# Neighbour sums by permutation matmuls: narrower one-hots in the first pass, and ten instead of eight destination blocks by row gathers

## The chip, the core and the metric

One core of a Trainium2 chip. The metric is device microseconds (us) of one execution. TensorE (PE in the profile) multiplies, VectorE (DVE) makes one-hot matrices by comparing keys with an index row, ScalarE (ACT) casts and empties PSUM (the memory that TensorE writes; the tiles that the other engines work on lie in SBUF), GpSimd (POOL) issues row gathers, and SyncE (SP) issues plain transfers.

## The reference, cut to what matters

```python
num_nodes, num_edges, dim = 4096, 65536, 128      # src, dst random node numbers
output = np.zeros((num_nodes, dim), dtype=np.float32)
for i in range(len(edge_index_src)):
    output[edge_index_dst[i]] += node_features[edge_index_src[i]]
```

## The kernel before: the parts that matter

Pass 1 sorts the edges into 32 destination blocks of 128 nodes. It does so in 24 lanes (six quads of four), each with 22 or 21 columns of 128 edges: it ranks the edges of a lane within their block, makes a one-hot of the rank (`p`), and moves each edge's code to the slot of its rank by matmuls. Then there are two ways to a destination block. Pass 2 sorts the edges of a block once more, by source block, builds for each source block a matrix of counts from two one-hots, and multiplies the 32 matrices by X; a turn of the main loop does this for one block and is called a slot. X is split into three bfloat16 terms side by side (`x3`, in DRAM `x3d`). The other way gathers, for every slot of pass 1, the row of `x3d`, and sums rows by one-hot matmuls. In the profile `psa` are the counts, `pso` the products with X, `psg` the sums of gathered rows, and `psr` the ranks of pass 2. Eight blocks go this way:

```python
KG = 8                          # blocks by gathers
GROUPS = (4, 4, 8, 8)           # the other 24, in groups of pass 2
GB = 6                          # row buffers

def gather(d, q):               # one unit: block d, quad q, four gathers
    t = xg.tile([P, 4, 3 * P], BF16, name="rows", tag="xg")
    for l in range(4):
        G.indirect_dma_start(out=t[:, l, :], out_offset=None, in_=x3d[:, :],
            in_offset=bass.IndirectOffsetOnAxis(ap=gidx[:, place(q).start + l, d:d + 1], axis=0))
# ... gather_sum: four matmuls of 128x384 into psg for each unit
def add_up(n):                  # gathers run at most GB units ahead of the sums
    while summed < min(n, ready):
        issue(summed + GB); gather_sum(*order[summed]); summed += 1
# ... the main loop: TensorE sums gathered units at the end of every slot
for slot, (g, i) in enumerate(flat_slots):
    n = n0 + (len(order) - n0) * (slot + 1) // slots
    # ... one-hots of the next slot on VectorE, steps of pass 2 of later groups
    for k in range(8):
        blocks(k, cur, a)                       # 4 matmuls, then a copy on ScalarE
        if prev is not None: product(k, prev[1], prev[2])   # 4 matmuls of 128x384
    # ...
    add_up(n)
finish()
for k in range(8): product(k, prev[1], prev[2])             # the last slot's products
```

At the start GpSimd zeroes those halves of the two `p2b` tiles that pass 2 never writes:

```python
p2b = [sb1.tile([P, NCH, P], BF16, name=f"p2b{i}") for i in range(2)]
for t in p2b:
    G.memset(t[:, :NH, 64:], 0.0)
    G.memset(t[:, NH:, :64], 0.0)
```

## Time and profile before

| | before |
|---|---|
| time, median (lowest to highest) | 368.02 us (366.36 to 368.76) |
| span of the profiled run | 366.4 us |
| busy PE / DVE / ACT / POOL | 82 / 78 / 44 / 61% |
| first gather starts, last gather ends | 49.19, 337.85 us |

The prediction below shows the lines, and reads them by stretch.

### The profile page before, as it was taken

The page shows a single profiled execution, that of the slowest core. Times are in us where ns is not written, and L with a number is a line of the kernel's source. Part 1 is how long each engine was busy: PE and PEld are TensorE (multiplying, and loading weights), DVE is VectorE, ACT ScalarE, POOL GpSimd, SP SyncE. Part 2 cuts the span into 40 slices and gives each one's busy share as a digit, 9 for nine tenths or more (in the row PEclk, how much of TensorE's full clock was granted, in tenths as well). Part 3 has the DMA queues.
Part 4 walks back from the last instruction along what each step waited for, and adds up shares of the span by engine and source line. Part 5 has one row for each costly group of instructions (what it writes and reads, how often), then busy time and mean ns, then how long its engine had stood idle before and what let it go on. Part 6 is the DMA issues. An engine that isn't in the chain of part 4 may idle for free.

```text
span 366.4 us, 8352 instructions
## 1 busy us (share of the span) xinstructions
PE 299.4 (82%) x3527; PEld 219.8 (60%) x3527; DVE 287.0 (78%) x476; ACT 160.2 (44%) x297; POOL 224.5 (61%) x225
## 2 busy tenths in 40 slices
PE   0768867656373597979989999997799999999996
PEld 0557746535351466756667767675477676767663
DVE  4982899999759689699994799659994959687721
ACT  2778733300000373525534553545345555464650
POOL 5677048787877777706887768578437575775000
PEclk9978988978565699989999999999899999999999
DMA  8400922233232233310324323232213332332000
GB/s 245 114 2 2 311 74 73 69 73 79 62 79 77 75 80 81 91 29 13 82 64 99 87 75 75 64 86 67 70 36 85 72 86 72 90 85 71 26 9 21
DMA packets 22694, 27.96 MB, mean 76 GB/s; under 512 B 3776, under 2 KB 19328, under 8 KB 22656
## 3 DMA queue, kind: packets, MB, share of 16 engines
q0 software_dynamic: 9216, 18.89, 21.2%
q1 hardware_dynamic: 13296, 8.01, 7.6%
q8 instruction: 27, 0.44, 0.5%
q10 hardware_dynamic: 144, 0.52, 0.4%
q14 instruction: 11, 0.09, 0.1%
HBM read 22.02 MB, written 5.39 MB: 75 GB/s over the span
## 4 chain that ended last, share of the span: by engine, by line
PE 55%; DVE 36%; ACT 5%; DMA 1%; issue 1%; DVEq 0%
PE pso L530 27%; DVE oh L196 10%; PE psa L524 9%; DVE p L196 8%; PE psg L325 6%; PE ps L496 4%; DVE cum L465 3%; DVE v L257 3%; DVE oh L442 3%; PE psr L474 3%; PE psb L449 2%; ACT cum L236 2%; DVE v L456 2%; PE psr L241 1%; ACT x L178 1%; DVE cum L470 1%
## 5 line engine op out<-in xcount | busy, mean ns | idle before, releaser
L306 POOL DMA_INDIRECT rows<-x3d,gidx x192 | 199.8, 1041 | 101.2 <-issue 48.1
L530 PE MATMUL pso<-x,a 128*128 128x384 bf16 x768 | 156.3, 328 | 5.5 <-DVE res L333 5.5
L526 ACT CAST a<-psa 128x512 bf16<-128x512 f32 x192 | 112.1, 586 | 77.5 <-PE psa L524 77.0
L530 PEld LDWEIGHTS <-a 128*128 128x128 bf16 x768 | 67.8, 98 | 32.1 <-issue 6.5
L524 PE MATMUL psa<-oh 128*128 128x128 bf16 x768 | 74.3, 220 | 1.2 <-ACT a L526 0.9
L524 PEld LDWEIGHTS <-oh 128*128 128x128 bf16 x768 | 59.0, 98 | 26.1 <-issue 2.5
L196 DVE TENSOR_TENSOR oh<-psi,slo 128x4096 bf16<-128x4096 uint16 x24 | 54.7, 2281 | 10.0 <-PE psa L524 10.0
L196 DVE TENSOR_TENSOR oh<-psi,dlo 128x4096 bf16<-128x4096 uint16 x24 | 54.7, 2278 | 0.0
L325 PE MATMUL psg<-rows,ohg 128*128 128x384 bf16 x192 | 40.2, 353 | 4.5 <-DMA rows<-x3d,gidx 3.0
L196 DVE TENSOR_TENSOR p<-psi,rank 128x2688 bf16<-128x2688 uint16 (+1 forms) x24 | 36.1, 1566 | 0.0
L325 PEld LDWEIGHTS <-ohg 128*128 128x128 bf16 x192 | 19.0, 104 | 17.1 <-DVE ohg L196 4.7
L504 DVE TENSOR_SCALAR slo<-pa 128x128 uint16<-128x128 uint16 x12 | 3.0, 252 | 32.8 <-ACT pa L500 32.8
L236 ACT ACTIVATE cum<-psc,minus 128x512 bf16<-128x512 f32 (+1 forms) x36 | 22.0, 656 | 12.2 <-PE psc L233 11.8
L182 POOL TENSOR_TENSOR xf<-xf,x 128x512 f32<-128x512 f32 x16 | 19.8, 1275 | 11.3 <-ACT x L178 11.3
L196 DVE TENSOR_TENSOR p2b<-psi,rank 128x768 bf16<-128x768 uint16 x48 | 23.3, 545 | 2.3 <-ACT rank L479 2.3
L280 PE MATMUL psm<-v,p 128*128 128x64 bf16 x512 | 20.6, 200 | 4.9 <-DVE p L196 4.8
L449 PE MATMUL psb<-oh,before 128*128 128x128 bf16 (+1 forms) x96 | 12.3, 309 | 14.7 <-DVE oh L442 11.8
L280 PEld LDWEIGHTS <-p 128*128 128x128 bf16 x512 | 18.6, 103 | 6.9 <-DVE p L196 6.5
L496 PEld LDWEIGHTS <-p2b 128*128 128x128 bf16 x576 | 19.7, 101 | 3.6 <-DVE p2b L196 2.1
L333 DVE TENSOR_REDUCE res<-pso 128x128 f32<-128x384 f32 x24 | 13.1, 546 | 10.0 <-PE pso L530 10.0
L233 PEld LDWEIGHTS <-sums 128*128 128x128 bf16 x126 | 12.1, 116 | 14.4 <-issue 6.6
L449 PEld LDWEIGHTS <-before 128*128 128x128 bf16 x96 | 10.0, 127 | 17.2 <-DVE oh L442 12.7
(72 smaller groups left out, 255.2 us busy)
## 6 DMA issues: line engine op xcount, KB each, us to landing
x3d<-x SPq DMA_DIRECT2D x4, 768.0 KB, 4.8
rows<-x3d,gidx POOLq DMA_INDIRECT x192
xf<-in_node_features_dram SPq DMA_DIRECT2D x4, 512.0 KB, 7.9
out_dram<-res SPq DMA_DIRECT2D x32, 64.0 KB, 1.9
raw<-in_edge_index_src_dram ACTq DMA_DIRECT2D x1, 512.0 KB, 5.2
raw<-in_edge_index_dst_dram SPq DMA_DIRECT2D x1, 512.0 KB
x3d<-zrow SPq DMA_DIRECT2D x1, 96.0 KB, 5.7
x3d<-zrow SPq DMA_DIRECT2D x1, 48.0 KB
```

Of the source, the lines that this page charges most:

```text
L182: G.tensor_tensor(out=xf[i][:, bs], in0=xf[i][:, bs], in1=part[:, bs], op=OP.add)
L196: V.tensor_tensor(out=dst.rearrange("p i (m k) -> p i m k", k=2), in0=io.rearrange("p i (m k) -> p i m k", k=2), in1=keys2[:, :, None, :]. ...
L236: S.activation(out=cum[:, :, 4 * j0:4 * (j0 + n)], func=RELU, bias=minus[:], in_=psc[:, :n * P].rearrange("p (t b) -> p b t", b=NB))
L280: PE.matmul(out=psm[:, l * 64:(l + 1) * 64], lhsT=p1[:, l % 2, j, :], rhs=v1[q][:, 4 * j + l].rearrange("p k b -> p (k b)"), start=j == 0, ...
L306: G.indirect_dma_start(out=t[:, l, :], out_offset=None, in_=x3d[:, :], in_offset=bass.IndirectOffsetOnAxis(ap=gidx[:, place(q).start + l, ...
L325: PE.matmul(out=psg[d][:, :3 * P], lhsT=oh[:, l, :], rhs=t[:, l, :], start=q == 0 and l == 0, stop=q == NQ - 1 and l == 3)
L333: V.tensor_reduce(out=res[:], in_=pso[:, :3 * P].rearrange("p (v f) -> p f v", v=3), op=OP.add, axis=AX.X, negate=True)
L449: PE.matmul(out=psb[:, h * W:(h + 1) * W], lhsT=before[:], rhs=flat2(oh2)[:, h * NH + c], start=c == 0, stop=c == NH - 1)
L496: PE.matmul(out=ps2[:, d % 2 * NB:(d % 2 + 1) * NB], lhsT=p2b[d % 2][:, c, :], rhs=v2[:, c, d // kk, :, d % kk], start=c == 0, stop=c == N ...
L524: PE.matmul(out=psa[:, i * P:(i + 1) * P], lhsT=oh[0][:, s, :], rhs=oh[1][:, s, :], start=True, stop=True)
L526: S.copy(out=a[:, k * 4:k * 4 + 4, :], in_=psa[:].rearrange("p (s m) -> p s m", s=4))
L530: PE.matmul(out=pso[:, :3 * P], lhsT=a[:, s, :], rhs=x3[:, s, :, :].rearrange("p v f -> p (v f)"), start=s == 0, stop=s == NB - 1)
```

## The change

The intent: compare only those ranks that a column of a lane can reach, and shift two blocks from TensorE and VectorE to GpSimd, which looks free. The prediction also weighs casts of X on ScalarE; the diff doesn't touch them. The diff, cut to its core (the rest rewrites pass 2 from generators to lists of steps with the same operations, and counts edges for the fallback's flag in another way):

```diff
-KG = 8
-GROUPS = (4, 4, 8, 8)
+KG = 10
+GROUPS = (4, 4, 8, 6)
+WIN = ((0, 7, 0, 64), (7, 14, 4, 100), (14, NJ, 20, P))
 ...
+    p1 = [sb1.tile([P, 2, NJ, P], BF16, name=f"p1{i}", tag=f"t2{i}") for i in range(2)]
+    for t in p1:
+        for j0, j1, m0, m1 in WIN:
+            if m0 > 0:
+                G.memset(t[:, :, j0:j1, :m0], 0.0)
+            if m1 < P:
+                G.memset(t[:, :, j0:j1, m1:], 0.0)
 ...
-            onehot(p1[:, l % 2, :n], rank1[q][:, l, :n], n)
+            for j0, j1, m0, m1 in WIN:
+                j1 = min(j1, n)
+                onehot(t[:, l % 2, j0:j1, m0:m1], rank1[q][:, l, j0:j1], j1 - j0, m1 - m0, m0=m0)
 ...
+                if l == 1 and q > 0:
+                    scan(q + 2)
+                if l > 0 or q == 0:
+                    count(q + 2, 2 if l < 3 else 99)
 ...
-        if q + 3 < NQ:
-            scan(q + 3)
```

More of the change, by code (lines that the diff above doesn't have):

```diff
@@ L25 @@
 BIG = 4096.0
-KG = 8
-GROUPS = (4, 4, 8, 8)
-STEPS = {0: [(1, 2)], 1: [(1, 2)], 2: [(1, 0)], 3: [(1, 0), (2, 1)], 4: [(2, 2)], 5: [(2, 1)],
-         6: [(2, 0)], 7: [(2, 0)], 9: [(2, 0), (3, 1)], 11: [(2, 0)], 12: [(3, 2)], 13: [(3, 1)],
-         14: [(3, 0)], 16: [(3, 0)], 18: [(3, 0)], 20: [(3, 0)]}
+KG = 10
+GROUPS = (4, 4, 8, 6)
+STEPS = {0: [(1, 2)], 1: [(1, 2)], 2: [(1, 1)], 3: [(1, 1), (2, 1)], 4: [(2, 2)], 5: [(2, 1)],
+         6: [(2, 1)], 7: [(2, 1)], 9: [(2, 1), (3, 1)], 11: [(2, 1)], 12: [(3, 2)], 13: [(3, 1)],
+         14: [(3, 1)], 16: [(3, 1)], 18: [(3, 1)]}
+WIN = ((0, 7, 0, 64), (7, 14, 4, 100), (14, NJ, 20, P))
 GE = 2
@@ L116, in _fast @@
     minus = sb1.tile([P, 1], F32, name="minus")
+    one = sb1.tile([P, 1], F32, name="one")
     iota = sb1.tile([P, P], U16, name="iota")
@@ L126, in _fast @@
     G.memset(minus[:], -BIG)
+    G.memset(one[:], 1.0)
     G.iota(iota[:], pattern=[[1, P]], base=0, channel_multiplier=0)
@@ L191, in _fast, with onehot @@
     oh1, sums, rank1, v1 = {}, {}, {}, {}
-    def onehot(dst, keys2, n, m=P, io=None):
-        io = (piota if io is None else io)[:, None, :m].to_broadcast([P, n, m])
+    def onehot(dst, keys2, n, m=P, io=None, m0=0):
+        io = (piota if io is None else io)[:, None, m0:m0 + m].to_broadcast([P, n, m])
         V.tensor_tensor(
@@ L273, in move1 @@
         for l in range(4):
-            if l % 2 == 0:
-                p1 = sb2.tile([P, 2, NJ, P], BF16, name="p1", tag="t2")
+            t = p1[l // 2]
             n = len([j for j in range(NJ) if j * NCH + q * 4 + l < T])
-            onehot(p1[:, l % 2, :n], rank1[q][:, l, :n], n)
+            for j0, j1, m0, m1 in WIN:
+                j1 = min(j1, n)
+                onehot(t[:, l % 2, j0:j1, m0:m1], rank1[q][:, l, j0:j1], j1 - j0, m1 - m0, m0=m0)
             meanwhile(l)
             for j in range(n):
-                PE.matmul(out=psm[:, l * 64:(l + 1) * 64], lhsT=p1[:, l % 2, j, :],
+                PE.matmul(out=psm[:, l * 64:(l + 1) * 64], lhsT=t[:, l % 2, j, :],
                           rhs=v1[q][:, 4 * j + l].rearrange("p k b -> p (k b)"),
@@ L393, in step @@
             if q + 2 < NQ:
-                count(q + 2, 2 if l < 3 else 99)
+                if l == 1 and q > 0:
+                    scan(q + 2)
+                if l > 0 or q == 0:
+                    count(q + 2, 2 if l < 3 else 99)
             if q == 0:
@@ L426, in pass2 @@
         shape = [P, NCH, gk, NB, kk]
-        if g == 0:
-            both = sb1.tile([P, 2] + shape[1:], BF16, name="vc2", tag="o0")
-            v2, cum2 = both[:, 0], both[:, 1]
-            oh2 = sb1.tile(shape, BF16, name="oh2", tag="o1")[:]
-        else:
-            oh2 = sb1.tile(shape, BF16, name="oh2", tag="c0")[:]
-            v2 = sb1.tile(shape, BF16, name="v2", tag="c1")[:]
-            cum2 = sb1.tile(shape, BF16, name="cum2", tag="o1")[:]
-        ds = slice(d0, d0 + gd)
         W = NB * gd
+        T2 = {}
@@ L438, in flat2 @@
         def flat2(t):
             return t.rearrange("p c i s k -> p c (i s k)")
-        for s in range(NB):
-            V.tensor_single_scalar(
-                out=oh2[:, :, :, s, :], in_=sbk[:, :, ds].rearrange("p c (i k) -> p c i k", k=kk),
-                scalar=float(s + 1), op=OP.is_equal)
-        yield
-        psb = ps.tile([P, 512], F32, name="psb", tag="misc", bufs=1)
-        for h in range(2):
-            for c in range(NH):
-                PE.matmul(out=psb[:, h * W:(h + 1) * W], lhsT=before[:],
-                          rhs=flat2(oh2)[:, h * NH + c], start=c == 0, stop=c == NH - 1)
@@ L451, in pass2 @@
-        for h in range(2):
-            S.copy(out=flat2(cum2)[:, h * NH], in_=psb[:, h * W:(h + 1) * W])
-        yield
-        for i in range(gk):
-            V.tensor_tensor(out=v2[:, :, i], in0=oh2[:, :, i], op=OP.mult,
-                            in1=sa[:, :, None, d0 + kk * i:d0 + kk * i + kk].to_broadcast(
-                                [P, NCH, NB, kk]))
-        yield
-        yield
-        cums = flat2(cum2).rearrange("p (h c) w -> p h c w", h=2)
-        ohs2 = flat2(oh2).rearrange("p (h c) w -> p h c w", h=2)
@@ L464, in pass2 @@
-        for c in range(1, NH):
-            V.tensor_tensor(out=cums[:, :, c], in0=cums[:, :, c - 1], in1=ohs2[:, :, c - 1],
-                            op=OP.add)
-        yield
-        yield
-        V.tensor_tensor(out=flat2(cum2), in0=flat2(cum2), in1=flat2(oh2), op=OP.mult)
-        yield
-        psr = ps.tile([P, 512], F32, name="psr2", tag="misc", bufs=1)
-        for s in range(NB):
-            PE.matmul(out=psr[:, :NCH * gd], lhsT=identb[:],
-                      rhs=cum2[:, :, :, s, :].rearrange("p c i k -> p (c i) k"),
-                      start=s == 0, stop=s == NB - 1)
@@ L477, in pass2, with tiles @@
-        rank2 = sb2.tile([P, gd, NCH, 2], BF16, name="rank2")
-        for k in range(2):
-            S.copy(out=rank2[:, :, :, k],
-                   in_=psr[:, :NCH * gd].rearrange("p (c d) -> p d c", d=gd))
-        yield
-        pa = sb2.tile([P, gd, NB], BF16, name="pa")
-        slo2 = sb2.tile([P, gd, NB, 2], U16, name="slo2")
-        dlo2 = sb2.tile([P, gd, NB, 2], U16, name="dlo2")
-        keys2[g] = (slo2, dlo2)
-        for i in range(0, gd, 2):
+        def tiles():
+            if g == 0:
+                both = sb1.tile([P, 2] + shape[1:], BF16, name="vc2", tag="o0")
+                T2["v"], T2["c"] = both[:, 0], both[:, 1]
+                T2["o"] = sb1.tile(shape, BF16, name="oh2", tag="o1")[:]
+            else:
+                T2["o"] = sb1.tile(shape, BF16, name="oh2", tag="c0")[:]
+                T2["v"] = sb1.tile(shape, BF16, name="v2", tag="c1")[:]
+                T2["c"] = sb1.tile(shape, BF16, name="cum2", tag="o1")[:]
@@ new lines, in buckets, with before_all @@
+        def buckets():
+            tiles()
+            ds = slice(d0, d0 + gd)
+            for s in range(NB):
+                V.tensor_single_scalar(
+                    out=T2["o"][:, :, :, s, :], scalar=float(s + 1), op=OP.is_equal,
+                    in_=sbk[:, :, ds].rearrange("p c (i k) -> p c i k", k=kk))
+        def before_all():
+            psb = ps.tile([P, 512], F32, name="psb", tag="misc", bufs=1)
+            for h in range(2):
+                for c in range(NH):
+                    PE.matmul(out=psb[:, h * W:(h + 1) * W], lhsT=before[:],
+                              rhs=flat2(T2["o"])[:, h * NH + c], start=c == 0, stop=c == NH - 1)
+            for h in range(2):
+                S.copy(out=flat2(T2["c"])[:, h * NH], in_=psb[:, h * W:(h + 1) * W])
@@ new lines, in payloads, with running @@
+        def payloads():
+            for i in range(gk):
+                V.tensor_tensor(out=T2["v"][:, :, i], in0=T2["o"][:, :, i], op=OP.mult,
+                                in1=sa[:, :, None, d0 + kk * i:d0 + kk * i + kk].to_broadcast(
+                                    [P, NCH, NB, kk]))
+        def running():
+            cums = flat2(T2["c"]).rearrange("p (h c) w -> p h c w", h=2)
+            ohs2 = flat2(T2["o"]).rearrange("p (h c) w -> p h c w", h=2)
+            for c in range(1, NH):
+                V.tensor_tensor(out=cums[:, :, c], in0=cums[:, :, c - 1], in1=ohs2[:, :, c - 1],
+                                op=OP.add)
@@ new lines, in masked, with ranks @@
+        def masked():
+            V.tensor_tensor(out=flat2(T2["c"]), in0=flat2(T2["c"]), in1=flat2(T2["o"]), op=OP.mult)
+        def ranks():
+            psr = ps.tile([P, 512], F32, name="psr2", tag="misc", bufs=1)
+            for s in range(NB):
+                PE.matmul(out=psr[:, :NCH * gd], lhsT=identb[:],
+                          rhs=T2["c"][:, :, :, s, :].rearrange("p c i k -> p (c i) k"),
+                          start=s == 0, stop=s == NB - 1)
+            T2["r"] = sb2.tile([P, gd, NCH, 2], BF16, name="rank2")
+            for k in range(2):
+                S.copy(out=T2["r"][:, :, :, k],
+                       in_=psr[:, :NCH * gd].rearrange("p (c d) -> p d c", d=gd))
@@ L488, in pass2, with permutations @@
+        def permutations(i):
+            if i == 0:
+                T2["pa"] = sb2.tile([P, gd, NB], BF16, name="pa")
+                keys2[g] = [sb2.tile([P, gd, NB, 2], U16, name=n) for n in ("slo2", "dlo2")]
             for d in range(i, i + 2):
@@ L490, in pass2, with permuted @@
                     cs = slice(h * NH, (h + 1) * NH)
-                    onehot(p2b[d % 2][:, cs, h * 64:h * 64 + 64], rank2[:, d, cs], NH, 64)
-            yield
+                    onehot(p2b[d % 2][:, cs, h * 64:h * 64 + 64], T2["r"][:, d, cs], NH, 64)
+        def permuted(i):
             ps2 = ps.tile([P, 512], F32, name="ps2", tag="misc", bufs=1)
@@ L496, in pass2, with pair_keys @@
                     PE.matmul(out=ps2[:, d % 2 * NB:(d % 2 + 1) * NB],
-                              lhsT=p2b[d % 2][:, c, :], rhs=v2[:, c, d // kk, :, d % kk],
+                              lhsT=p2b[d % 2][:, c, :], rhs=T2["v"][:, c, d // kk, :, d % kk],
                               start=c == 0, stop=c == NCH - 1)
-            ds = slice(i, i + 2)
-            S.copy(out=pa[:, ds], in_=ps2[:, :2 * NB].rearrange("p (d s) -> p d s", d=2))
-            yield
-            pau = pa[:, ds].bitcast(U16).rearrange("p d s -> p (d s)")[:, :, None].to_broadcast(
-                [P, 2 * NB, 2])
-            V.tensor_single_scalar(out=slo2[:, ds].rearrange("p d s k -> p (d s) k"), in_=pau,
-                                   scalar=7, op=OP.logical_shift_right)
-            V.tensor_single_scalar(out=dlo2[:, ds].rearrange("p d s k -> p (d s) k"), in_=pau,
-                                   scalar=127, op=OP.bitwise_and)
+            S.copy(out=T2["pa"][:, i:i + 2],
+                   in_=ps2[:, :2 * NB].rearrange("p (d s) -> p d s", d=2))
+        def pair_keys(i):
+            pau = T2["pa"][:, i:i + 2].bitcast(U16).rearrange("p d s -> p (d s)")[
+                :, :, None].to_broadcast([P, 2 * NB, 2])
+            for t, arg, op in zip(keys2[g], (7, 127), (OP.logical_shift_right, OP.bitwise_and)):
+                V.tensor_single_scalar(out=t[:, i:i + 2].rearrange("p d s k -> p (d s) k"),
+                                       in_=pau, scalar=arg, op=op)
             if i == 0:
-                V.tensor_reduce(out=fmax[:, NQ + g:NQ + 1 + g], in_=rank2[:, :, :, 0], op=OP.max,
+                V.tensor_reduce(out=fmax[:, g:g + 1], in_=T2["r"][:, :, :, 0], op=OP.max,
                                 axis=AX.XY)
-            yield
+        pairs = [tuple(lambda f=f, i=i: f(i) for f in (permutations, permuted, pair_keys))
+                 for i in range(0, gd, 2)]
+        return [(buckets, before_all), (payloads,), (running,), (masked, ranks)] + pairs
     def onehots(g, i):
-        oh = sb2.tile([P, 2, NB, P], BF16, name="oh", tag="t2")
+        oh = sb1.tile([P, 2, NB, P], BF16, name="oh", tag=f"t2{(first[g] + i) % 2}")
         for k, io in ((0, piotas), (1, piota)):
@@ L534, in flag @@
     def flag():
-        for q in range(NQ):
-            V.tensor_reduce(out=fmax[:, q:q + 1], in_=rank1[q][:, :, :, 0], op=OP.max, axis=AX.XY)
-        V.tensor_single_scalar(out=fmax[:, :NQ], in_=fmax[:, :NQ], scalar=-64.0, op=OP.add)
+        ng = len(GROUPS)
+        full = sb1.tile([P, NCH * NB], BF16, name="full", tag="o2")
+        V.tensor_single_scalar(out=full[:], in_=sbk[:].rearrange("p c b -> p (c b)"), scalar=0.5,
+                               op=OP.is_gt)
+        V.tensor_reduce(out=fmax[:, ng:ng + 1], in_=full[:], op=OP.add, axis=AX.X)
@@ L539, in flag @@
+        V.tensor_scalar(out=fmax[:, :ng], in0=fmax[:, :ng], scalar1=63.5, scalar2=float(2 * P * T),
+                        op0=OP.is_gt, op1=OP.mult)
         fall = sb1.tile([P, 1], F32, name="fall")
-        V.tensor_reduce(out=fall[:], in_=fmax[:, :NQ + len(GROUPS)], op=OP.max, axis=AX.X)
+        V.tensor_reduce(out=fall[:], in_=fmax[:, :ng + 1], op=OP.add, axis=AX.X)
         psf = ps.tile([P, 512], F32, name="psf", tag="misc", bufs=1)
-        PE.transpose(out=psf[:1, :P], in_=fall[:], identity=ident[:])
@@ L543, in flag @@
-        fone = sb1.tile([1, 1], F32, name="fone")
-        V.tensor_reduce(out=fone[:], in_=psf[:1, :P], op=OP.max, axis=AX.X)
-        V.tensor_single_scalar(out=flag_i[:], in_=fone[:], scalar=63.5, op=OP.is_gt)
-    gens = [pass2(g) for g in range(len(GROUPS))]
-    def on(g):
-        next(gens[g])
-    pending = []
-    on(0)
-    on(0)
-    serve(NQ - 1)
-    for _ in range(2):
-        on(0)
-        on(0)
-    on(0)
-    on(0)
-    add_up(8)
-    on(0)
-    on(0)
-    ready = len(order)
@@ L566, in _fast, with run @@
-    on(0)
-    prepare(10)
-    on(0)
-    oh = onehots(0, 0)
-    on(0)
-    add_up(10)
-    on(0)
-    prev = None
+        PE.matmul(out=psf[:1, :1], lhsT=fall[:], rhs=one[:], start=True, stop=True)
+        V.tensor_single_scalar(out=flag_i[:], in_=psf[:1, :1], scalar=float(P * T),
+                               op=OP.not_equal)
+    todo = [pass2(g) for g in range(len(GROUPS))]
+    def run(fs):
+        for f in fs:
+            f()
+    run(todo[0].pop(0))
+    serve(NQ - 1)
+    for _ in range(3):
+        run(todo[0].pop(0))
@@ L574, in _fast @@
+    add_up(9)
+    vec, mat, keys = todo[0].pop(0)
+    vec()
+    mat()
+    ready = len(order)
+    prepare(12)
+    keys()
+    vec, mat, keys = todo[0].pop(0)
+    vec()
+    oh = onehots(0, 0)
+    mat()
+    keys()
+    add_up(12)
+    prev = None
+    pending = []
     n0 = summed
@@ L577, in _fast @@
     for slot, (g, i) in enumerate(flat_slots):
-        steps = STEPS.get(slot, ())
         n = n0 + (len(order) - n0) * (slot + 1) // slots
-        for pg in pending:
-            on(pg)
-        pending = [pg for pg, k in steps if k == 0]
+        run(pending)
+        steps = [todo[pg].pop(0) for pg, k in STEPS.get(slot, ()) for _ in range(k)]
+        pending = [f for st in steps for f in st[2:]]
         prepare(n)
@@ L586, in _fast @@
             oh = onehots(*flat_slots[slot + 1])
-        for pg, k in steps:
-            for _ in range(max(k - 1, 0)):
-                on(pg)
-                on(pg)
-            on(pg)
+        run(st[0] for st in steps)
         finish()
@@ L600, in _fast @@
             done.append((prev[0], prev[2]))
-        for pg, k in steps:
-            on(pg)
+        run(st[1] for st in steps if len(st) > 1)
         add_up(n)
```

## The prediction

> **What bounds the kernel now.** I read the chain that ended last first, to see which engine sets the end; then the stretches of 20 us, to see where each engine is full; then GpSimd's timeline, because the change gives GpSimd a quarter more of its one long job.
>
> The page's busy shares and chain:
>
> ```profile
> PE 299.4 (82%) x3527; PEld 219.8 (60%) x3527; DVE 287.0 (78%) x476; ACT 160.2 (44%) x297; POOL 224.5 (61%) x225
> ...
> PE 55%; DVE 36%; ACT 5%; DMA 1%; issue 1%; DVEq 0%
> ```
>
> TensorE carries over half of the chain, VectorE a third, GpSimd nothing. The stretches (busy us of PE, PEld, DVE, ACT, POOL, then clock, DMA share, GB/s):
>
> ```profile
> 60.00:80.00 20.00, 11.76 (x231) 9.51 (x232) 19.73 (x24) 4.96 (x12) 15.73 (x15) 0.85 0.30 74
> 100.00:120.00 20.00, 11.31 (x138) 7.57 (x135) 14.87 (x26) 0.83 (x4) 15.14 (x16) 0.59 0.33 80
> 300.00:320.00 20.00, 20.00 (x212) 14.22 (x210) 16.32 (x18) 10.89 (x20) 13.33 (x15) 1.00 0.30 80
> ```
>
> So pass 1 (about 38 to 86 us) is VectorE's, the setup of pass 2 (to about 115) is latency with no full engine, and from about 200 us TensorE has no gap. GpSimd shows 13 to 16 of 20 us and looks free. It isn't quite; the groups and its timeline say why:
>
> ```profile
> L306 POOL DMA_INDIRECT rows<-x3d,gidx x192 | 199.8, 1041 | 101.2 <-issue 48.1 <-PE psg L325 34.3 <-DVE gkey L296 12.4
> ```
>
> ```profile
> 49.19 1.10 POOL L306 DMA_INDIRECT rows<-x3d,gidx  x1 [12.40 <-DVE gkey L296]
> ...
> 155.46 0.95 POOL L306 DMA_INDIRECT rows<-x3d,gidx  x1 [0.30 <-issue]
> 167.53 4.51 POOL L306 DMA_INDIRECT rows<-x3d,gidx  x1 [11.12 <-PE psg L325]
> ...
> 181.47 3.94 POOL L306 DMA_INDIRECT rows<-x3d,gidx  x1 [0.30 <-issue]
> 185.72 0.95 POOL L306 DMA_INDIRECT rows<-x3d,gidx  x1 [0.30 <-issue]
> 186.97 0.94 POOL L306 DMA_INDIRECT rows<-x3d,gidx  x1 [0.30 <-issue]
> ```
>
> A gather is 0.95 us plus a gap of 0.30 that nothing fills: one every 1.25 us, and the gap is not counted as busy. The stream begins at 49.19 and ends at 337.85, 288.7 us. It splits into 191 steps of 1.25 plus a last 0.95 (239.7), 18 us by which some gathers were longer than 0.95 (my sum over all of them), and some 31 us of waits for TensorE to free a row buffer (11.1, 8.9 and seven small ones). Those 31 us and the 17 us from the last unit's bytes to the matmuls that use it (340 to 357) are all the slack that GpSimd has.
>
> **What the Trainium skill says.** "SBUF — State Buffer", section "SBUF: two separate sides", says that VectorE and GpSimd share a port pair as an exclusive lock, and that while VectorE runs an instruction that holds it, GpSimd cannot write DMA descriptors. The trace agrees: VectorE's mask multiply (L470, 128x6144, all in SBUF) runs from 181.25 to 184.60, and the gather begun at 181.47 takes 3.94 instead of 0.95. The one-hot compares, whose index row lies in PSUM, leave gathers at 0.95. "Perfetto Trace Analysis", section "DMA Instruction — SWDGE (GPSIMD)", says that such an instruction's recorded end is the last descriptor, not the data: here the queues move bytes until about 158.0 after a gather that ended at 156.41, and until about 340 after 337.85, so rows land 1.6 to 2.1 us later. "TensorE: Matmul & The Clock Gate", section "Part 1: The HAM clock gate", has the clock halve after an idle window of about 3.4 us and come back after as much work; here TensorE's idle 159.7 to 162.1 is followed by a granted clock of 0.50 from 163 to 166.
>
> **The change part by part.**
>
> *Pass 1 one-hots.* 24 compares of 2816 or 2688 elements (means 1611 and 1544 ns; four back to back take 5.84, so 1.46 apiece in pace) become 72 over windows of 7x64, 7x96 and 8x108: 1984 elements, or 1876 where there are 21 columns, about 70%. From the paces of the 4096- and 2688-element compares (2.20 and 1.46) an element costs 0.526 ns and an instruction about 0.06 us fixed. The three cost 1876 x 0.526 + 0.18 = 1.17, so 0.3 is saved per lane, 1.2 per quad, 7 us in the six. Quad 0's is hidden behind ScalarE; about 6 us lie on VectorE's path. I worked out every slot of the drawn edges from the reference's inputs: ranks are 0 to 49, 14 to 84 and 35 to 110 in the three windows, so none falls outside and the fallback isn't taken.
>
> *Scans.* VectorE sits 7.4 us before the scan at 37.60, waiting for column sums that TensorE reaches only after quad 0. Moved into the next quad after its second compare, the scan lets two of quad 1's four compares run in that hole, some 2.5 to 3.4 us. Later quads hardly wait there (0.25).
>
> *Zeroing the windows' margins.* 3328 elements on GpSimd in 16 memsets; by p2b's 0.73 for 768 about 3.4 us, in a stretch where it idles 3.35 before the first subtraction. No cost.
>
> *Casts of X.* The diff leaves them as they are, already 12 ScalarE instructions of 1.07 us. Nothing.
>
> *The flag.* Six reduces (1.0 us) become a compare and a reduce over 768. Even.
>
> *Two blocks from products to gathers.* Slots go from 24 to 22. Each slot removed takes from TensorE 8 x 0.87 = 7.0 us (psa and pso); the pair takes one permutation (1.5 us) too: 15.5. Added are 48 matmuls of 128x384 at 0.163: 7.8. Net 7.7 us less in a stretch where TensorE is full. VectorE loses 8.8 of slot one-hots, 1.9 of p2b and a quarter of the last group's work, and gains 12 x 0.37.
>
> So TensorE and VectorE alone would bring 367.7 to about 367.7 - 6 - 3 - 7.7 = 351. But GpSimd gets 48 more gathers, 60 us at 1.25, against 48 us of slack, of which the faster engines take away more. So its stream should set the end:
> - Start: the first gather needs x3d written. The writes fill the queues until 47.1 (329 GB/s at 45) and are bound by bandwidth, so 49.2 becomes about 47, not less.
> - 240 gathers without a wait: 239 x 1.25 + 0.95 = 299.7.
> - Longer gathers behind VectorE's port: 18 us now. Instructions that fell in GpSimd's waits (the 192-element bucket compares at 158, the multiply at 264) will now hit a running stream, the last group is a quarter smaller: about 19.
> - So the last gather ends at 47 + 299.7 + 19 = 365.7, and lands at 367.7.
> - The tail: from the last four psg matmuls (357.20) to the end of the span (366.4) is 9.2 now, with the final 32 products behind them: 376.9.
> - In the last slot TensorE waits for three units at 5 us each, so the final products should start at half clock: 1.8 more, 378.7.
> - Measured times lie 1.3 to 1.8 above the span: about 380. I take 379.
>
> Do the buffers keep the stream from stalling? Gather units per slot go from 38/24 = 1.6 to 48/22 = 2.2, so 8.7 gathers or 10.9 us a slot, against TensorE's 7.0 + 0.75 + 2.2 x 0.65 = 9.2. Through the first slots, where TensorE now takes 10 to 12, the stream is six buffers ahead: unit 24, say, is issued near 177 and needs unit 18 summed, done before 166 in today's slot 3. So I expect hardly a wait for TensorE, and TensorE waiting instead.
>
> **The rivals.** (a) *TensorE stays the bound*: 351. For it: the chain shows no GpSimd, and its busy share is 61%. Against it: the share leaves out the 0.30 gaps, and even with no blocked gather 47 + 299.7 + 11.2 + 1.5 = 359.4 is a floor. (b) *Fewer blocked gathers*: if the rearranged VectorE stream meets only 12 us of them and the clock holds, 370, within 2%. For it: how much one such instruction costs varied from 0.6 (multiply at 77.58) to 3.6 us (167.5). (c) *The half clock spreads*: if the per-slot wait of about 2 us grew past some 2.5, each slot's matmuls would slow, but the gathers leave room for that, so it adds a few us at most: 383 to 386. (d) *The fallback runs*: many times slower, ruled out by the ranks unless the count is wrong.
>
> **Range and chances.** The certain part is 299.7 + 11.2 + 1.5 = 312.4; the start (46 to 49), blocking (14 to 23) and final clock (0 to 2) give 372 to 386. I take 371 to 386. Slower than 375.1 (2%) needs start plus blocking plus final clock above 62.7, where I expect 67: 0.80. Faster than 360.4 needs almost no blocking: 0.02.
>
> **What would show it.** Right: GpSimd's gathers at 1.25 us without a wait from about 47 to 366, waits for psg near zero, TensorE idle before psg for rows in most slots from the sixth on, the chain of waits with GpSimd in it, the 72 compares taking about 29 us of VectorE against 36.1 now, final products at a clock under 1. Wrong: gathers closer than 1.25, a stream that still waits for TensorE, TensorE full after 200 us, or an end near 351.

## The result, and the profile after

The changed kernel takes 388.18 us (385.48 to 390.54, 4 runs) against 368.02: slower. The ratio is 1.055, with a 95% interval of 1.046 to 1.065. Ratios here are the mean time of one kernel's runs over that of the other's of the same rounds, so not quite the ratio of the medians. Executions over 1.5% slower than the fastest of the same kernel are left out of the means. All runs are correct; the fallback was not taken.

The direction and the mechanism were as predicted, but the time lies 2.2 us above the top of the range. The four runs fall in two pairs, 385.48 and 386.12, 390.23 and 390.54, and the profile is of the third. The page's busy shares and the chain that ended last (followed back from the last instruction, at each step to what released it), after:

```profile
PE 308.1 (79%) x3400; PEld 217.5 (56%) x3400; DVE 275.4 (71%) x522; ACT 150.2 (39%) x280; POOL 280.1 (72%) x282
...
PE 50%; DVE 15%; POOL 11%; issue 9%; DMA 9%; ACT 6%; ACTq 0%; DVEq 0%
```

GpSimd, its gaps ("issue") and the gathers' transfers, which had 2% of the chain, now have 29%, and VectorE's 36% have become 15%. The stretches (busy us of PE, PEld, DVE, ACT, POOL, then clock, DMA share, GB/s):

```profile
60.00:80.00 20.00, 13.09 (x229) 10.12 (x227) 17.04 (x38) 4.95 (x12) 15.74 (x14) 0.88 0.29 70
...
240.00:260.00 20.00, 15.43 (x106) 9.48 (x106) 10.23 (x12) 6.43 (x11) 15.13 (x17) 0.83 0.37 88
...
300.00:320.00 20.00, 20.00 (x248) 14.37 (x245) 14.67 (x22) 9.78 (x18) 15.13 (x17) 1.00 0.36 87
320.00:340.00 20.00, 16.54 (x142) 11.00 (x141) 13.07 (x14) 9.13 (x16) 15.12 (x17) 1.00 0.38 89
```

VectorE does have less to do in pass 1 (17.0 of 20 us against 19.7), but TensorE is no longer full in every stretch after 200 us. GpSimd shows 15.1 us in stretch after stretch: 16 gathers at 1.25 us fill 20 us, and 16 x 0.947 = 15.15 is what counts as busy. So 15.1 of 20 is a GpSimd that has no time left. The groups and who waited for whom, in two views:

```profile
L320 POOL DMA_INDIRECT rows<-x3d,gidx x240 | 250.8, 1045 | 83.6 <-issue 62.1
```

```profile
POOL rows L320 <- issue: 62.1, 204, 0.3
...
PE psg L339 <- DMA rows<-x3d,gidx: 29.9, 37, 1.9
```

The entry "PE psg 34.3" of before is gone from the gathers' row: GpSimd does not wait for TensorE any more. In its place TensorE waits 29.9 us for gathered rows.

Along GpSimd's stream the two kernels can be compared term by term. "Longer gathers" is the sum over all gathers of what they take above 0.948 us, and "waits" the sum of idle time above 0.30 before gathers other than the first:

| us | before | after | predicted for after |
|---|---|---|---|
| first gather starts | 49.19 | 51.36 | 47 |
| gathers and gaps alone | 239.8 | 299.8 | 299.7 |
| longer gathers | 18.1 | 23.7 | 19 |
| waits | 30.8 | 0.1 | 0 |
| last gather ends (the sum) | 337.85 | 375.00 | 365.7 |
| from there to the end of the span | 28.6 | 13.5 | 13.0 |
| span | 366.4 | 388.5 | 378.7 |

The 48 more gathers cost 60.0 us. The waits (30.7) and the slack at the end (15.1) gave 45.8 of that back; the start (2.2) and the longer gathers (5.6) added. That makes 22 us of span. Two terms were mis-sized, the start by 4.4 us and the longer gathers by 4.7.

**The start.** VectorE's first instructions, before and then after:

```profile
5.90 0.57 DVE L157 TENSOR_SCALAR kd<-raw 128x176 uint16<-128x176 uint16 x3 [2.88 <-DMA raw<-in_edge_index_dst_dram]
6.39 1.62 DVE L196 TENSOR_TENSOR oh<-psi,kd 128x2816 bf16<-128x2816 uint16 x1
7.92 0.42 DVE L163 TENSOR_SCALAR raw<-raw 128x528 uint16<-128x528 uint16 x1
```

```profile
5.87 1.87 DVE L170 TENSOR_SCALAR kd<-raw 128x176 uint16<-128x176 uint16 x3 [2.81 <-DMA raw<-in_edge_index_dst_dram]
7.67 1.60 DVE L209 TENSOR_TENSOR oh<-psi,kd 128x2816 bf16<-128x2816 uint16 x1
9.19 1.32 DVE L176 TENSOR_SCALAR raw<-raw 128x528 uint16<-128x528 uint16 x1
```

The same three shifts take 1.87 us instead of 0.57, and the next key operation 1.32 instead of 0.42. GpSimd's memsets at that time:

```profile
6.03 0.83 POOL L153 MEMSET p2b<- 128x768 bf16 x1
6.81 0.83 POOL L154 MEMSET p2b<- 128x768 bf16 x1
7.59 0.83 POOL L153 MEMSET p2b<- 128x768 bf16 x1
8.37 0.73 POOL L154 MEMSET p2b<- 128x768 bf16 x1
```

The new memsets come first, so the old ones, which used to end at 5.68 just before the keys arrived, now lie on top of VectorE's shifts. The one-hot compare, whose index row is in PSUM, takes its 1.60 as before. The delay then runs on: ScalarE makes the codes at 12.12 instead of 9.12, and the first write of `x3d` is issued at 38.49 instead of 35.91.

### The profile page after: what moved, and what is told of

It is laid out like the page before. It is cut to its first block, busy times and chain, and to the rows that moved or that the text cites. A ratio compares the mean times of both kernels' runs of the same rounds, so it can differ in the third digit from the quotient of the medians.

```text
span 388.5 us, 8206 instructions
## 1 busy us (share of the span) xinstructions
PE 308.1 (79%) x3400; PEld 217.5 (56%) x3400; DVE 275.4 (71%) x522; ACT 150.2 (39%) x280; POOL 280.1 (72%) x282
## 4 chain that ended last, share of the span: by engine, by line
PE 50%; DVE 15%; POOL 11%; issue 9%; DMA 9%; ACT 6%; ACTq 0%; DVEq 0%
PE pso L552 22%; POOL rows L320 11%; PE psa L546 8%; DMA rows<-x3d,gidx 8%; PE psg L339 5%; ACT cum L249 3%; DVE oh L209 3%; DVE p L209 2%; PE psr L254 2%; PE ps L515 2%; PE psb L470 2%; PE psr L494 2%; DVE oh L462 2%; PE psm L294 2%; PE psc L246 2%
## 5 line engine op out<-in xcount | busy, mean ns | idle before, releaser
L320 POOL DMA_INDIRECT rows<-x3d,gidx x240 | 250.8, 1045 | 83.6 <-issue 62.1
L552 PE MATMUL pso<-x,a 128*128 128x384 bf16 x704 | 150.7, 341 | 3.3 <-DVE res L347 3.3
L548 ACT CAST a<-psa 128x512 bf16<-128x512 f32 x176 | 102.6, 585 | 120.4 <-PE psa L546 118.0
L339 PE MATMUL psg<-rows,ohg 128*128 128x384 bf16 x240 | 55.8, 352 | 35.0 <-DMA rows<-x3d,gidx 29.9
L209 DVE TENSOR_TENSOR oh<-psi,slo 128x4096 bf16<-128x4096 uint16 x22 | 50.2, 2282 | 14.2 <-PE psa L546 14.2
L209 DVE TENSOR_TENSOR oh<-psi,dlo 128x4096 bf16<-128x4096 uint16 x22 | 50.1, 2279 | 0.0
L339 PEld LDWEIGHTS <-ohg 128*128 128x128 bf16 x240 | 23.5, 102 | 46.6 <-issue 30.9
L209 DVE TENSOR_TENSOR p<-psi,rank 128x448 bf16<-128x448 uint16 (+3 forms) x72 | 29.2, 479 | 0.0
L209 DVE TENSOR_TENSOR ohg<-psi,gkey 128x512 bf16<-128x512 uint16 x60 | 22.1, 412 | 0.0
L242 PE MATMUL psc<-oh,early 128*128 128x512 bf16 (+1 forms) x36 | 14.9, 414 | 3.2 <-ACT cum L249 3.2
```

The costliest lines, as they stand in the source:

```text
L209: V.tensor_tensor(out=dst.rearrange("p i (m k) -> p i m k", k=2), in0=io.rearrange("p i (m k) -> p i m k", k=2), in1=keys2[:, :, None, :]. ...
L242: PE.matmul(out=psc[:, :n * P], lhsT=early[:], rhs=oh1q(q)[:, 4 * j0:4 * (j0 + n), :].rearrange("p t b -> p (t b)"), start=True, stop=j0 + ...
L339: PE.matmul(out=psg[d][:, :3 * P], lhsT=oh[:, l, :], rhs=t[:, l, :], start=q == 0 and l == 0, stop=q == NQ - 1 and l == 3)
L548: S.copy(out=a[:, k * 4:k * 4 + 4, :], in_=psa[:].rearrange("p (s m) -> p s m", s=4))
L552: PE.matmul(out=pso[:, :3 * P], lhsT=a[:, s, :], rhs=x3[:, s, :, :].rearrange("p v f -> p (v f)"), start=s == 0, stop=s == NB - 1)
```

## The experiments

Ten kernels ran, all with correct results. Times are medians of all runs, with the ratio to the kernel before of the same rounds.

| run | what | time | ratio (95% interval) |
|---|---|---|---|
| e1_rest_only | the change without the two blocks | 362.67 | 0.985 (0.980 to 0.990) |
| e2_gathers_only | the two blocks without the rest | 385.05 | 1.044 (1.038 to 1.050) |
| e3_zero_later | change, p2b zeroed later | 383.74 | 1.041 (1.036 to 1.046) |
| e4_last_sums_last | change, last sums after the last products | 380.94 | 1.033 (1.026 to 1.040) |
| e5_short_multiplies | change, multiplies of pass 2 in pieces | 384.55 | 1.044 (1.038 to 1.050) |
| e6_nine_blocks | nine blocks, zeroed later | 365.52 | 0.987 (0.979 to 0.996) |
| e7_eight_blocks | eight blocks, zeroed later | 360.12 | 0.978 (0.973 to 0.984) |
| e8_ten_all | ten blocks with e3, e4 and e5 | 377.19 | 1.024 (1.019 to 1.029) |
| e9_nine_all | nine blocks with e3, e4 and e5 | 365.41 | 0.991 (0.985 to 0.996) |
| e10_eight_short | e7 with short multiplies | 364.96 | 0.989 (0.984 to 0.993) |

The theory: GpSimd's stream of gathers sets the end. First rival: the rest of the change does.

**e1_rest_only**

```diff
-KG = 10
-GROUPS = (4, 4, 8, 6)
+KG = 8
+GROUPS = (4, 4, 8, 8)
-         ... 18: [(3, 1)]}
+         ... 18: [(3, 1)], 20: [(3, 1)]}
```

> The changed kernel with 8 gathered blocks as before (groups 4, 4, 8, 8): windows, moved scan, new flag and the reordered program alone. Theory (the 48 added gathers carry the loss; the stream of row gathers sets the end): with 192 gathers the stream has slack again, the end goes back to TensorE, and the time is 358 to 365 us: 6 us of shorter compares and up to 3 from the scan, less some 2.6 us that the longer zeroing costs early on; GpSimd waits for TensorE 20 us or more in all. Rival (the reordered program of pass 2 and the windows cost the time): it stays above 375 us.

Measured: 362.67 us. The rest of the change is worth 5 us. GpSimd waits again, 15.2 us in all above the gaps; this is under the 20 that I named. The largest entry in the view of who waited for whom (with the gaps in it) reads so:

```profile
POOL rows L320 <- PE psg L339: 17.4, 8, 8.1
```

**e2_gathers_only**

```diff
 # the kernel before
-KG = 8
-GROUPS = (4, 4, 8, 8)
+KG = 10
+GROUPS = (4, 4, 8, 6)
-         ... 18: [(3, 0)], 20: [(3, 0)]}
+         ... 18: [(3, 0)]}
```

> The kernel before with 10 gathered blocks (groups 4, 4, 8, 6) and nothing else of the change. Theory: first gather near 49.2, then 299.7 us of stream plus 20 to 25 us of blocked gathers, 13.5 us of tail, so a span of 383 to 388 and a time of 384 to 390 us, with hardly a wait of GpSimd for TensorE. Rival (the loss lies in the rest of the change): below 372 us.

Measured: 385.05 us. First gather at 50.09, longer gathers 20.1, waits 0.2, last gather ends at 370.64, span 383.3. The two blocks alone cost 17 us. The rival falls: the loss is theirs. The whole change is even slower than this, by 3 us, although its other parts gain 5 us with eight blocks: where the gather stream sets the end, quicker one-hots have nothing to shorten, and a first gather 1.3 us later and longer gathers (23.7 us against 20.1) lengthen the stream one for one.

**e3_zero_later**

```diff
-    for t in p2b:
-        G.memset(t[:, :NH, 64:], 0.0)
-        G.memset(t[:, NH:, :64], 0.0)
 ...
     for q in range(NQ):
         move1(q, during(q))
+        if q == 0:
+            for t in p2b:
+                G.memset(t[:, :NH, 64:], 0.0)
+                G.memset(t[:, NH:, :64], 0.0)
```

> The changed kernel with the zeroing of the p2b tiles moved behind the first subtractions, so that GpSimd zeroes only the p tiles in the first 6 us. Theory (the longer zeroing on GpSimd holds VectorE's key shifts back by the shared port, and the delay of about 3 us runs through codes, ranks and casts to the writes of x3d and so to the first gather): the kd shifts are back at 0.2 to 0.3 us each in place of 0.6, the first gather starts at 48 to 49 in place of 51.4, and the time falls by about 2.5 us to 384 to 387. Rival (the first gather is late for another reason, for instance the moved scan): the first gather stays at 51 or later.

Measured: 383.74 us (381.69 to 386.66), a little under the range that I gave. VectorE's first instructions are back:

```profile
5.76 0.75 DVE L167 TENSOR_SCALAR kd<-raw 128x176 uint16<-128x176 uint16 x3 [2.69 <-DMA raw<-in_edge_index_dst_dram]
6.43 1.61 DVE L206 TENSOR_TENSOR oh<-psi,kd 128x2816 bf16<-128x2816 uint16 x1
7.96 0.42 DVE L173 TENSOR_SCALAR raw<-raw 128x528 uint16<-128x528 uint16 x1
```

The first gather starts at 48.70, 2.7 us earlier than in the change, though the scan stayed where the change put it. The three shifts take 0.57 to 0.75 us in all six profiles with this edit (e3, e6 to e10) and 1.82 to 1.98 in the four of the changed program without it (the change, e1, e4, e5). The first gather starts at 47.74 to 50.48 with it and at 50.39 to 51.36 without, 2.2 us later on average. So the memsets caused most of the late start, but the start also varies by itself, by up to 2.7 us. This is the other side of the lock that the prediction quotes: a memset on GpSimd holds back VectorE just as VectorE holds back gathers.

**e4_last_sums_last**

```diff
-        add_up(n)
+        if slot < slots - 1:
+            add_up(n)
 ...
     for k in range(8):
         product(k, prev[1], prev[2])
+    add_up(n)
     done.append((prev[0], prev[2]))
     finish()
```

> The changed kernel with the last three units of gathered rows summed after the final 32 products in place of before them. Theory (the stream of gathers sets the end, and the final products, 7.8 us at a low clock, only come behind it): the gathers end where they did, near 375, and the time falls by 7 to 8 us, to about 380. Rival (TensorE's own work sets the end): the time stays within 2 us of 388.

Measured: 380.94 us, as expected, though the gathers did not end where they did: the last one ends at 371.25, not near 375. TensorE at the end, first in the changed kernel and then in this one:

```profile
375.55 0.48 PE L339 MATMUL psg<-rows,ohg 128*128 128x384 bf16 x1 [0.69 <-DMA rows<-x3d,gidx]
377.04 0.48 PE L339 MATMUL psg<-rows,ohg 128*128 128x384 bf16 x1 [1.02 <-DMA rows<-x3d,gidx]
377.31 7.83 PE L552 MATMUL pso<-x,a 128*128 128x384 bf16 x32
```

```profile
364.81 6.01 PE L552 MATMUL pso<-x,a 128*128 128x384 bf16 x36
370.66 1.95 PE L339 MATMUL psg<-rows,ohg 128*128 128x384 bf16 x11
373.28 0.32 PE L339 MATMUL psg<-rows,ohg 128*128 128x384 bf16 x1 [0.67 <-DMA rows<-x3d,gidx]
```

In the change TensorE waits for single rows and only then does its last 32 products, and slowly: 7.83 us against 5.36 in the kernel before, with a granted clock of 0.50 until 382.3. Here the products are done while the gathers come in. From the last gather's end (371.25) to the end of the span it is 7.15 us in place of 13.5. The profiled span falls by 10.1 us, more than the medians' 7.2; what the tail leaves of it is the longer gathers, which are 20.1 us in this profile and 23.7 in that of the change; this edit can't have caused that, so some of it is spread from run to run.

**e5_short_multiplies**

```diff
-                V.tensor_tensor(out=T2["v"][:, :, i], in0=T2["o"][:, :, i], ...)
+                for c in range(0, NCH, 3):
+                    V.tensor_tensor(out=T2["v"][:, c:c + 3, i], in0=T2["o"][:, c:c + 3, i], ...)
 ...
-            V.tensor_tensor(out=flat2(T2["c"]), in0=flat2(T2["c"]), in1=flat2(T2["o"]), op=OP.mult)
+            for c in range(0, NCH, 2):
+                V.tensor_tensor(out=flat2(T2["c"])[:, c:c + 2], ...)
```

> The changed kernel with the payload multiplies and the mask multiplies of pass 2 cut into pieces of 256 to 512 elements (8 or 12 pieces for one), the same numbers otherwise. About 10 to 12 of the 20 to 24 us by which gathers are longer than 0.95 us fall on these multiplies. Theory (a gather waits for the end of the one VectorE instruction that holds the shared port, then gets in): the sum of the excess falls to 10 to 15 us and the time by 6 to 10 us, to 378 to 382. Rival (VectorE keeps the port from one short instruction to the next, as the 32 bucket compares seem to): the excess stays at 20 us or more and the time at 385 or more.

Measured: 384.55 us, between theory and rival, and the longer gathers sum to 18.6 us. The gathers beside the pieces of the payload multiply (166) and of the mask multiply (181.8 on), in GpSimd's timeline:

```profile
166.04 5.03 POOL L320 DMA_INDIRECT rows<-x3d,gidx  x1 [0.30 <-issue]
...
181.76 1.10 POOL L320 DMA_INDIRECT rows<-x3d,gidx  x1 [0.30 <-issue]
183.16 1.04 POOL L320 DMA_INDIRECT rows<-x3d,gidx  x1 [0.30 <-issue]
184.51 1.03 POOL L320 DMA_INDIRECT rows<-x3d,gidx  x1 [0.30 <-issue]
```

Both happened. Between the 12 mask pieces (0.34 us apart) the gathers got in, where the whole multiply had held one for 3.04 us. Beside the 16 payload pieces (0.27 apart) one gather was held until they were through, 5.03 us. The form of the piece doesn't decide it. In this same run eight payload pieces at 121.95 let a gather through in 1.04 us, and the last group's mask pieces, from 278.13, let one through in 1.01 and held the next for 2.39. In e10 sixteen payload pieces like those at 166 let two through from 245.49 on (1.06 and 1.04) and held the third for 2.18. What decides it stays open.

**e6_nine_blocks.** The last group of pass 2 keeps eight blocks, overlaps the one before by one block, and that block gets no second slot.

```diff
-KG = 10
-GROUPS = (4, 4, 8, 6)
+KG = 9
+GROUPS = (4, 4, 8, 8)
-         14: [(3, 1)], 16: [(3, 1)], 18: [(3, 1)]}
+         14: [(3, 1)], 15: [(3, 1)], 17: [(3, 1)], 19: [(3, 1)]}
-    first = [KG + sum(GROUPS[:g]) for g in range(len(GROUPS))]
+    first = [9, 13, 17, 24]
-    flat_slots = [... for i in range(gd)]
+    flat_slots = [... for i in range(gd) if (g, i) != (3, 0)]
 # and the edit of e3
```

> The changed kernel with 9 gathered blocks, 23 slots (the last group of 8 overlaps the one before by a block that gets no slot), and the zeroing of p2b moved behind the first subtractions. Theory (the end is the later of two: TensorE's work and the stream of gathers): the stream ends near 48.7 + 269.7 + 22 = 340, so it allows a time of 353; TensorE's work is that of 8 blocks, 362.7, less 2.6 for the zeroing and 3 for the slot: 357. So 356 to 360, the best so far. Rival (each gathered block costs time, as from 8 to 10): above 364.

Measured: 365.52 us (360.40 to 366.59): missed, and on the rival's side of 364, though one run is at 360.40. The profiled run counts as slow, being 1.7% above the fastest of its four, so its profile is only a hint: no waits of GpSimd for TensorE, longer gathers 29.8 us, last gather ends at 350, TensorE waits 12 us for rows in all.

**e7_eight_blocks.** e1 with the edit of e3.

> As e1, 8 gathered blocks, with the zeroing of p2b moved behind the first subtractions. Theory: TensorE sets the end and the 2.6 us of the earlier start reach it: 359 to 361.5. Rival (the slack later swallows the earlier start): 362 to 363 as without.

Measured: 360.12 us, as expected: where TensorE sets the end, a start earlier by 2.6 us (47.80 against 50.39 in e1) also reaches it, because pass 1 lies on VectorE's and ScalarE's path too: the first slot starts at 115.3 us against 117.6. This is the best version, 2.2% below the kernel before, though its interval (0.973 to 0.984) does not lie wholly beyond 2%.

**e8_ten_all.** The edits of e3, e4 and e5 together.

> The changed kernel, 10 blocks, with all three: zeroing later, the last sums last, short multiplies. Theory: the three act on separate terms of one sum (start, blocked gathers, tail), so they add: 388.2 - 4.4 - 7.2 - 6 to 10 gives 366 to 371, which is no better than the kernel before, because 240 gathers at 1.25 us are 300 us whatever else is done. Rival (TensorE takes over as the bound once the stream is shorter): 372 or more, with GpSimd waiting for TensorE.

Measured: 377.19 us, and no wait of GpSimd (0.1 us). So the number missed and the rival that would explain it is not what happened. In the profile the terms do add: start 47.74, 299.8, longer gathers 19.2, so a last gather at 366.84, and 7.16 to the end make 374.0, which is the span. What was wrong is my sum: I took 6 to 10 us for the short multiplies, whose own run shows 3.6, and added up gains of medians; that each of them held some of the same spread of longer gathers is likely, but not shown. The rest of its claim stands: not even with all three do 240 gathers come under the kernel before.

**e9_nine_all.** e6 with the edits of e4 and e5.

> Nine gathered blocks with zeroing later, the last sums last and short multiplies. The run with nine blocks missed its 356 to 360 (365.5; GpSimd never waited, and gathers were longer by 29.8 us in sum, so the stream ended at 350 and not at 340). Theory (at nine blocks the stream and TensorE are so close that each gather blocked by VectorE shows up): with the excess at 20 to 24 and the sums last the stream ends near 342 and the time is 356 to 361. Rival (the slots as rearranged for nine blocks cost TensorE the time): 364 or more although the stream ends early.

Measured: 365.41 us. The stream ended early (last gather at 339.4, longer gathers 19.2), as the theory wanted, and the time did not follow. So the rival's side: TensorE or VectorE ran late. The next run says how much of that comes with the short multiplies.

**e10_eight_short.** e7 with the edit of e5.

> Eight gathered blocks with zeroing later and short multiplies. Theory (with eight blocks TensorE sets the end and blocked gathers cost nothing): 359 to 361.5, the 360.1 of the run without the short multiplies. Rival (blocked gathers still delay TensorE by late rows or late buffers): 357 or less.

Measured: 364.96 us, 4.8 us slower than e7; neither was right. The matmuls that add up ranks wait for the mask multiply. In the view of who waited for whom, e7 and then e10 (total, times, longest):

```profile
PE psr L495 <- DVE cum L490: 1.1, 3, 0.7
```

```profile
PE psr L498 <- DVE cum L492: 5.7, 2, 3.1
```

By these matmuls e10 lags e7 by 2.3 us at the first group's, 2.3, 3.6 and 5.5 us at the last one's (259.39 and 264.85), and the spans differ by 5.5. VectorE is busy 5.6 us longer (287.1 against 281.5). So the pieces' fixed cost is paid on TensorE's path: pass 2's steps on VectorE lie between the slots and are not hidden. In e5, where TensorE waited for gathers anyway, this would not show. In e9 the same wait is 4.6 us against 1.1 in e6, which fits that nine blocks with short multiplies gained nothing. Why nine blocks without them stayed at 365.5 remains open; its profile is one of a slow run, and nine blocks with few blocked gathers and long multiplies were not run. In that profile the first slot starts at 120.7 us, in e7 at 115.3, of which 2.7 us are a later first gather (50.48); from the first slot's start to the last one's it takes 226.8 us with 23 slots, where e7 takes 225.5 with 24. So the slot that was saved didn't shorten the loop.

## Why the prediction was right or wrong

- **The mechanism, 48 more gathers at 1.25 us against 48 us of slack: right.** Gathers and gaps take 299.8 us, as worked out, GpSimd does not wait for TensorE (0.1 us), and e1 and e2 put the loss on the two blocks.
- **"So 49.2 becomes about 47, not less": this step failed**, by 4.4 us, in two ways. I took the end of the bytes of `x3d`'s write (47.1) for the time at which a gather may start. But before, the bytes stop near 47.1 and the gather starts at 49.19; after, they stop near 49.4 and it starts at 51.36. So 2 us from a write's last byte to the first gather belong in the sum, the same 2 us that I did count for the rows. The other 2.2 us are the next point.
- **"No cost" of zeroing the margins: wrong.** I counted only whether GpSimd itself had time (and 16 memsets where there are 8, with the elements right). Its memsets held VectorE's shifts back by the shared ports, and e3 won 2.7 us of start by moving them, and 4.4 us of median time, which is more than the start can give and so in part spread. I had quoted the lock, but only in the one direction.
- **Longer gathers of 19 us: mis-sized**, 23.7 in the profiled run. I had expected that the multiplies and compares that used to fall into GpSimd's waits would now hit gathers, and they did, but gave it 1 us. The term is also loose: 20.1 in e2, 22.8 in e3, 20.1 in e4. The profiled run of the change, at 390.23 us, is one of the two longer of the four.
- **The tail of 13.0 us: right** (13.5). The half clock cost 2.5 us instead of 1.8; e4 shows that 6.4 of the 13.5 are avoidable.
- **Pass 1: right in size.** The 72 compares take 29.2 us against 36.1 (29 predicted), and e1 shows the gain when TensorE sets the end. There the whole rest of the change gave 5 us, and another 2.5 once the memsets were out of the way (e7). The size is in part luck: the two paces give a fixed cost of 0.05 us an instruction, not 0.06, and so a gain of 8 us where 7 was written and 6.9 measured. What the moved scan alone is worth was not run apart.
- **Rival (a), TensorE stays the bound near 351: didn't come**, as expected with ten blocks. With eight, where TensorE does set the end, 360 was reached (e7).
- **The other rivals.** (b), only 12 us of longer gathers: 23.7 came. (c), the half clock spreads: it did come in the main loop (194.6 to 201.4 and 252.6 to 259.4), after waits of at most 1.1 us between single matmuls, where the prediction wanted 2.5; but GpSimd waited 0.1 us in all, so it did not lengthen the stream. (d), the fallback: not taken.

With the start at 51.4 and longer gathers at 23.7 in the sum, the predicted span of 378.7 becomes 387.8, and with the 0.5 us of tail 388.3, against 388.5 measured.

## What to carry to other kernels

An engine's busy share can hide that it has no time left: take the pitch of its repeated instruction, gap included, times the count, and compare it with the time that is there before you give it more work. Where two engines share ports, ask in both directions who holds whom back, above all for cheap instructions put into an "idle" stretch. And measure a cure where the engine it burdens sets the end, not where that engine is waiting: the short multiplies looked good with ten blocks and cost 4.8 us with eight.

## What the Trainium skill lacked or had wrong

- "SBUF — State Buffer", section "SBUF: two separate sides": it gives the lock as held for one whole instruction, and has a blocked DMA go on some 115 ns after VectorE's end. Here one gather was held for 5.03 us beside 16 instructions of 0.27 us each (e5), and in the changed kernel for 4.26 us by 32 compares that together took 3.65; in other places gathers got in between short instructions (1.03 to 1.10 us beside 12 multiplies of 0.34). What decides whether the ports pass over between two instructions is not stated. The section also has a VectorE instruction with two SBUF inputs lock out only a GpSimd operation that reads SBUF. The multiply of 128x6144, both inputs in SBUF, held a gather for 3.94 us (before, at 181.47); whether a gather, whose row numbers lie in SBUF, counts as such a read is not said there.
- "DMA: Bandwidth & Descriptors": I found no pitch for indirect gathers. Here one gather of 128 rows of 768 bytes takes 0.95 us of GpSimd and a gap of 0.30 where nothing blocks it.
- "TensorE: Matmul & The Clock Gate", section "Part 1: The HAM clock gate": its table has the clock halve after an idle window of about 3.4 us; further on it says that frequent short idles do so too, but not how short. Here an idle time of 2.4 us was enough for a granted clock of 0.50 (before, 159.7 to 162.1), and in the changed kernel single matmuls with waits of at most 1.34 us between them led to 0.50 from 375.5 to 382.3.
